# A hybrid decoder layer: attention values 13 or 14 steps behind their scores, eight heads in one softmax, norm weights moved into the rotary tables and the keys

## The chip, the core and the metric

The kernel runs on one core of one Trainium2 chip. The core has a matrix engine (PE, with its weight loads shown as PEld), a vector engine (DVE), a scalar engine (ACT), a general engine (POOL) and SP, which here only issues DMAs. Each engine works through its own instructions in order; they wait for one another through semaphores. Times are device microseconds of one execution, from repeated runs of the same program. The profile comes from one further execution that was recorded by the hardware.

## The reference

One layer of a decoder on 256 tokens of width 2048, in float32. The part that matters here is the attention half of the first mixing block: 32 query heads of 64 dimensions, 8 key and value heads, a window of 128 tokens in two blocks of 128 queries, and a learned sink per head.

```python
qh = _rmsnorm(q.reshape(b, s, ATT_HEADS, ATT_HEAD_DIM), q_norm_g[i])
kh = _rmsnorm(k.reshape(b, s, ATT_KV_HEADS, ATT_HEAD_DIM), k_norm_g[i])
qh = _partial_rope(qh, cos, sin)
kh = _partial_rope(kh, cos, sin)
...
sc = jnp.einsum('bnqhrd,bnkhd->bnhrqk', qb, kb) * scale
sc = jnp.where(mask[None, :, None, None], sc, -jnp.inf)
m = jnp.maximum(jnp.max(sc, axis=-1, keepdims=True), sink)
e = jnp.exp(sc - m)
pr = e / (jnp.sum(e, axis=-1, keepdims=True) + jnp.exp(sink - m))
o = jnp.einsum('bnhrqk,bnkhd->bnqhrd', pr, vb)
```

Around it stand the state-space half of the same block, the output projection that both halves feed, a gated feed-forward part and a small embedding part.

## The kernel before

Nearly all the work is products of 256 token rows with big float32 weights. Each weight tile of 128x1024 is loaded into a raw buffer `w` (`WR` = 6 of them), then split into a high part `wh` (a cast on ACT, L192) and the rest `wl` (a subtraction on DVE, L193), with `WB` = 4 buffers each. One such tile is one **step**: twelve matmuls of 128x512 on PE (L219 to L221: high by high, low weights by high, high weights by low, for two k tiles and two token blocks). A raw buffer comes free when DVE has made `wl` from it; `wh` and `wl` come free when PE has done their step.

The attention stage is written as 104 steps, numbered from 0, and PE's order in it is written by hand: q(0) is steps 0 to 7, the keys 8 to 15, the values' projection 16 to 23, q(1) 24 to 31, output(1) 32 to 39, q(2) 40 to 47, output(2) 48 to 55, q(3) 56 to 63, and output(3) to output(7) fill steps 64 to 103. A table `at` hangs the attention products behind certain steps. The other engines' order is set by a scheduler.

The queries come in four groups j of eight heads, two key heads (kv) each. For each group and each block b of 128 queries the chain is this:

- `norm_rope` takes the projected queries from the accumulators (ACT, L607), squares them (ACT, L609), sums per head (DVE, L611), takes the power -1/2 on POOL (L187, called from `rstd`), scales (DVE, L613), multiplies by the norm's weights (POOL, L614, 128x512), and turns the first 16 dimensions (POOL, six small instructions, L621 to L623).
- `flipped` transposes float32 through its two 16-bit halves: a copy into `half` (POOL for queries and keys, ACT for probabilities), a DMA transpose issued by SP (L631), and a copy from `flip` on POOL (L632). The result is `qT`, `kT`, or the probabilities `s` themselves, transposed in place. There are two `half` and two `flip` buffers for all of them.
- `scores(j, b, kv)` makes four heads: PE (L679) into one PSUM tile `sc`, mask added on DVE (L680), maximum (L687), minimum with the sink (L688), four exponentials on ACT (L691), the denominator (L693 to L696), the scaling (DVE, L697), then `flipped`. A group takes four such calls, two with 128 keys (b = 0) and two with 256 (b = 1).
- `values(j)` multiplies the transposed probabilities with `v` on PE (L712) and splits the result into `yT`, the left side of output(4 + j).

SP issues weight loads (L207) and transposes (L631) from one queue, in order. A projection's result is added from its accumulators to the residual by DVE (L359); there are two pairs of accumulators, so PE can start a block of two steps when DVE has added the block before the last.

Of the kernel before, what the change touches and what calls it, by code (L numbers as in the profile page):

```python
# [20 lines left out]
P = 128  # L21
# [6 lines left out]
KG = 4  # L28
KW = 2
WB = 4  # L30
WR = 6
LINE = 512

HD = 64
# [31 lines left out]
def hybrid_layer(  # L66
# [64 lines left out]
    hp = ctx.enter_context(tc.tile_pool(name="hp", bufs=1))  # L131
    hres = [sb(hp, [P, D], f"h{b}") for b in range(NB)]
    mix = ExitStack()
    yp_ = mix.enter_context(tc.tile_pool(name="yp", bufs=4))
    xin_ = ExitStack()
    xin = xin_.enter_context(tc.tile_pool(name="xin", bufs=1))
    gn = sb(const, [P, 4 * KT], "gains")
# [151 lines left out]
    def v3(a, m):  # L289
        return a.rearrange("p (a b) -> p a b", a=m)  # L290
# [308 lines left out]
    with tc.tile_pool(name="att_s", bufs=2) as as_, tc.tile_pool(name="att", bufs=2, reuse_waits="tile") as ap_, tc.tile_pool(name="ps_sc", bufs=1, space=PSUM) as ps_sc:  # L599
# [2 lines left out]
        nsink = sb(as_, [P, 32], "nsink", bufs=1)  # L602
        V.tensor_scalar_mul(nsink, sink, -1.0)

        def norm_rope(acc, b, gain, tag):
            r = sb(ap_, [P, NC], "qkr", bufs=1)
            S.activation(out=r, in_=acc[b], func=AF.Copy, scale=rx[:, b : b + 1])  # L607
            n = sb(ap_, [P, NC], "qkn")
            S.activation(out=n, in_=r, func=AF.Square)  # L609
            ss = sb(as_, [P, 8], "ss8")  # L610
            V.tensor_reduce(out=ss, in_=v3(n, 8), axis=AX.X, op=ALU.add)  # L611
            rs = rstd(ss, HD, 8, "rs8")
            V.tensor_tensor(out=v3(r, 8), in0=v3(r, 8), in1=bc(rs, HD), op=ALU.mult)  # L613
            G.tensor_tensor(out=v3(n, 8), in0=v3(r, 8), in1=gain.unsqueeze(1).to_broadcast([P, 8, HD]), op=ALU.mult)  # L614
            n3 = v3(n, 8)
            a, c_ = n3[:, :, :HALF], n3[:, :, HALF:ROPE]
            cs = cos_t[:, b, :].unsqueeze(1).to_broadcast([P, 8, HALF])
            sn = sin_t[:, b, :].unsqueeze(1).to_broadcast([P, 8, HALF])
            t = [sb(as_, [P, 8, HALF], f"rot{i}", bufs=1) for i in range(4)]
            for i, (u_, w_) in enumerate(((a, cs), (c_, sn), (c_, cs), (a, sn))):  # L620
                G.tensor_tensor(out=t[i], in0=u_, in1=w_, op=ALU.mult)  # L621
            G.tensor_tensor(out=a, in0=t[0], in1=t[1], op=ALU.subtract)
            G.tensor_tensor(out=c_, in0=t[2], in1=t[3], op=ALU.add)  # L623
            return n

        def flipped(dst, n, put):

# [11 lines left out]
        def queries(j, acc):  # L639
            qTs[j] = []  # L640
            for b in range(NB):
                n = norm_rope(acc, b, qscaled, "q")
# [5 lines left out]

        def keys(acc):
            for b in range(NB):  # L650
                n = norm_rope(acc, b, kg_, "k")
# [15 lines left out]

        probs = {}

        def scores(j, b, kv):  # L670

            W = (b + 1) * P
            qT = qTs[j][b]
            s = sb(ap_, [P, 4, W], f"s{b}")
            sc = ps_sc.tile([P, 4, 2 * P], F32, tag="sc", name=nm("sc"))[:, :, :W]
            for i in range(2):
                for e in range(2):
                    es = slice(e * HD, (e + 1) * HD)
                    PE.matmul(sc[:, 2 * e + i, :], lhsT=qT[es, kv * 2 + i, :], rhs=kT[es, 2 * j + kv, :W], start=True, stop=True)  # L679
            V.tensor_tensor(out=s, in0=sc, in1=band[:, 2 * P - W :].unsqueeze(1).to_broadcast([P, 4, W]), op=ALU.add)  # L680
            h0 = j * 8 + kv * 4

            def pairs(a):
                return a[:, h0 : h0 + 4].rearrange("p (i e) -> p e i", e=2)

            nm_ = sb(as_, [P, 4], "nm")
            V.tensor_reduce(out=nm_, in_=s, axis=AX.X, op=ALU.max, negate=True)  # L687
            V.tensor_tensor(out=v3(nm_, 2), in0=v3(nm_, 2), in1=pairs(nsink), op=ALU.min)  # L688
            den = sb(as_, [P, 4], "den")
            for h in range(4):  # L690
                S.activation(out=s[:, h, :], in_=s[:, h, :], func=AF.Exp, bias=nm_[:, h : h + 1], accum_out=den[:, h : h + 1])  # L691
            es_ = sb(as_, [P, 4], "es")
            V.tensor_tensor(out=v3(es_, 2), in0=v3(nm_, 2), in1=pairs(sink), op=ALU.add)  # L693
            S.activation(out=es_, in_=es_, func=AF.Exp)
            V.tensor_tensor(out=den, in0=den, in1=es_, op=ALU.add)
            V.reciprocal(den, den)  # L696
            V.tensor_tensor(out=s, in0=s, in1=bc(den, W), op=ALU.mult)  # L697
            p = s.rearrange("p h w -> p (h w)")
            flipped(p.rearrange("p (c t) -> p c t", t=P), 4 * W, lambda half: S.copy(half, halves(p)))
            probs[j, b, kv] = s.rearrange("p h (k t) -> p h k t", t=P)  # L700

        def values(j):

            yT = Lhs(yp_, KG, "y")
            for b in range(NB):
                o = tr_tile()
                for kv in range(2):
                    pT = probs.pop((j, b, kv))
                    vs = slice((2 * j + kv) * HD, (2 * j + kv + 1) * HD)
                    for kb in range(b + 1):  # L710
                        for e in range(2):
                            PE.matmul(  # L712
                                v3(o[e * HD : (e + 1) * HD, kv * 2 * P : (kv + 1) * 2 * P], 2),
                                lhsT=v[kb][:, vs],
                                rhs=pT[:, 2 * e : 2 * e + 2, kb, :],
                                start=(kb == 0),
                                stop=(kb == b),
                                skip_group_check=True,
                            )
                hi, lo = (t[:, :, b * P : (b + 1) * P] for t in yT.t[0])  # L720
                split(v3(o, 4), hi, lo)
            held[4 + j] = (yT, w_out, 4 + j, 1)
# [211 lines left out]
```

## Time and profile before

| what | value |
|---|---|
| median of 3 runs | 1462.4 us (1461.29 to 1462.82) |
| the profiled execution | 1464.43 us, its span 1462.7 us |
| mean granted TensorE clock | 0.992 |
| ACT busy | 793.1 us (54%) |
| POOL busy | 307.1 us (21%) |
| HBM traffic | 268.32 MB read, 2.13 MB written |

The span is the time from the first to the last instruction in the trace; the execution's own time is 1.7 us more. Waits are listed by the engine that waits and by what came last; a wait counts for the total only where it is PE's, since PE is busy nearly all the time. Matmuls are pipelined: one of 128x512 is shown with 0.39 us, but the next one starts 0.23 us later, so their spacing is read from start to start.

### The profile page before, as it was taken

The page shows a single profiled execution, that of the slowest core. Times are in us where ns is not written, and L with a number is a line of the kernel's source. Part 1 is how long each engine was busy: PE and PEld are TensorE (multiplying, and loading weights), DVE is VectorE, ACT ScalarE, POOL GpSimd, SP SyncE. Part 2 cuts the span into 40 slices and gives each one's busy share as a digit, 9 for nine tenths or more (in the row PEclk, how much of TensorE's full clock was granted, in tenths as well). Part 3 has the DMA queues.
Part 4 walks back from the last instruction along what each step waited for, and adds up shares of the span by engine and source line. Part 5 has one row for each costly group of instructions (what it writes and reads, how often), then busy time and mean ns, then how long its engine had stood idle before and what let it go on. Part 6 is the DMA issues. An engine that isn't in the chain of part 4 may idle for free.

```text
span 1462.7 us, 18060 instructions
## 1 busy us (share of the span) xinstructions
PE 1431.3 (98%) x6516; PEld 1167.7 (80%) x6516; DVE 1000.7 (68%) x1262; ACT 793.1 (54%) x1075; POOL 307.1 (21%) x246
## 2 busy tenths in 40 slices
PE   9999999999979899999999999999999999999998
PEld 6787888888757667888888888888888888888887
DVE  6668876767868697775666755774675576476854
ACT  6675555544546564565655545544554564455653
POOL 0002010029444350102334202311320231020000
PEclk9999999999989999999999999999999999999999
DMA  9665665556875686758778768767776877676672
GB/s 336 211 190 184 201 189 172 174 158 200 200 191 148 189 199 167 207 185 226 209 211 221 215 197 217 214 204 204 211 222 196 212 209 216 202 211 188 212 221 85
DMA packets 163595, 292.62 MB, mean 200 GB/s; under 512 B 93169, under 2 KB 96049, under 8 KB 163121
## 3 DMA queue, kind: packets, MB, share of 16 engines
q1 hardware_dynamic: 163072, 290.99, 68.6%
q8 instruction: 51, 0.84, 0.2%
q10 hardware_dynamic: 432, 0.48, 0.1%
q14 instruction: 40, 0.32, 0.1%
HBM read 268.32 MB, written 2.13 MB: 185 GB/s over the span
## 4 chain that ended last, share of the span: by engine, by line
PE 88%; DMA 4%; DVE 4%; POOL 2%; ACT 1%; issue 1%; SPq 0%; DVEq 0%; POOLq 0%; ACTq 0%
PE acc L219 27%; PE acc L220 27%; PE acc L221 27%; DMA flip<-half 2%; DVE wl L193 1%; PE ms L495 1%; PE acc L318 1%; PE acc L319 1%; PE acc L317 1%; PE tr L252 1%; DMA w<-in_w_in_dram 1%; ACT wh L192 1%; PE tr L712 1%; POOL s L632 1%; PE sc L679 1%
## 5 line engine op out<-in xcount | busy, mean ns | idle before, releaser
L193 DVE TENSOR_TENSOR wl<-w,wh 128x1024 fp32r<-128x1024 f32 (+1 forms) x493 | 640.3, 1303 | 364.3 <-ACT wh L192 363.1
L192 ACT CAST wh<-w 128x1024 fp32r<-128x1024 f32 (+1 forms) x493 | 515.2, 1048 | 496.7 <-PE acc L221 446.6
L220 PE MATMUL acc<-wl,ah 128*128 128x512 f32 x1280 | 500.9, 391 | 1.4 <-DVE wl L193 1.4
L221 PE MATMUL acc<-wh,al 128*128 128x512 f32 x1280 | 500.6, 391 | 0.0
L219 PE MATMUL acc<-wh,ah 128*128 128x512 f32 x1280 | 499.9, 392 | 0.0
L220 PEld LDWEIGHTS acc<-wl,ah 128*128 128x128 f32 x1280 | 241.1, 188 | 52.2 <-DVE wl L193 2.2
L219 PEld LDWEIGHTS acc<-wh,ah 128*128 128x128 f32 x1280 | 241.1, 188 | 52.1 <-issue 2.4
L221 PEld LDWEIGHTS acc<-wh,al 128*128 128x128 f32 x1280 | 240.9, 188 | 50.2 <-issue 0.5
L221 PE MATMUL acc<-wh,gl 128*128 128x512 f32 x352 | 137.0, 389 | 0.0
L220 PE MATMUL acc<-wl,gh 128*128 128x512 f32 x352 | 137.0, 389 | 0.0
L219 PE MATMUL acc<-wh,gh 128*128 128x512 f32 x352 | 136.4, 389 | 0.0
L814 POOL COPY half<-u 128x1024 uint16<-128x1024 uint16 x44 | 61.4, 1407 | 262.5 <-ACT u L812 262.5
L219 PE MATMUL acc<-wh,yh 128*128 128x512 f32 x256 | 102.1, 399 | 1.9 <-DVE h L359 1.9
L220 PE MATMUL acc<-wl,yh 128*128 128x512 f32 x256 | 100.2, 391 | 0.0
L221 PE MATMUL acc<-wh,yl 128*128 128x512 f32 x256 | 99.8, 391 | 0.0
L817 POOL COPY uc<-flip 128x1024 uint16<-128x1024 uint16 x44 | 56.4, 1281 | 169.2 <-DMA flip<-half 169.2
L220 PEld LDWEIGHTS acc<-wl,gh 128*128 128x128 f32 x352 | 66.1, 188 | 13.7
L221 PEld LDWEIGHTS acc<-wh,gl 128*128 128x128 f32 x352 | 66.1, 188 | 13.7
L219 PEld LDWEIGHTS acc<-wh,gh 128*128 128x128 f32 x352 | 66.1, 188 | 13.6
L359 DVE TENSOR_TENSOR h<-h,acc 128x512 f32<-128x512 f32 x112 | 73.3, 678 | 3.6 <-PE acc L221 3.6
L268 DVE SCALAR_TENSOR_TENSOR cv<-uc,fcw,cv 128x254 f32<-128x254 f32 (+1 forms) x176 | 73.2, 477 | 3.4 <-ACT cv L266 3.4
L219 PEld LDWEIGHTS acc<-wh,yh 128*128 128x128 f32 x256 | 48.3, 189 | 16.2 <-issue 3.8
(225 smaller groups left out, 1160.4 us busy)
## 6 DMA issues: line engine op xcount, KB each, us to landing
w<-in_w_up_dram SPq DMA_DIRECT2D x176, 512.0 KB, 4.1
w<-in_w_in_dram SPq DMA_DIRECT2D x126, 512.0 KB, 4.1
w<-in_w_down_dram SPq DMA_DIRECT2D x88, 512.0 KB, 4.3
w<-in_w_out_dram SPq DMA_DIRECT2D x64, 512.0 KB, 4.2
w<-in_w_pg_dram SPq DMA_DIRECT2D x32, 512.0 KB, 4.3
seg<-scr SPq DMA_DIRECT2D x8, 512.0 KB, 5.1
xt<-in_xT_dram SPq DMA_DIRECT2D x16, 128.0 KB, 7.1
h<-in_x_dram SPq DMA_DIRECT2D x2, 1024.0 KB, 8.4
```

The source lines that it names most:

```text
L192: S.copy(hi, src)
L193: V.tensor_tensor(out=lo, in0=src, in1=hi.bitcast(F32), op=ALU.subtract)
L219: PE.matmul(acc[b], lhsT=hi, rhs=wh[:, i, :], start=(k == 0), stop=False)
L220: PE.matmul(acc[b], lhsT=hi, rhs=wl[:, i, :], start=False, stop=False)
L221: PE.matmul(acc[b], lhsT=lo, rhs=wh[:, i, :], start=False, stop=(k == total - 1))
L252: PE.transpose(tr[:, i, b * P : (b + 1) * P], src[b][:, f * P : (f + 1) * P], ident)
L268: V.scalar_tensor_tensor(out=dst[:, s:], in0=ps[:, : T - s], scalar=taps[n - 1 - s], in1=dst[:, s:], op0=ALU.mult, op1=ALU.add)
L317: PE.matmul(acc[b], lhsT=h, rhs=wh[:, c, :], start=(k == 0), stop=False)
L318: PE.matmul(acc[b], lhsT=h, rhs=wl[:, c, :], start=False, stop=False)
L359: V.tensor_tensor(out=hs, in0=hs, in1=acc[b], op=ALU.add)
L814: G.tensor_copy(half.rearrange("p (a n) -> p a n", a=2), u_.bitcast(U16).rearrange("p (n a) -> p a n", a=2))
L817: G.tensor_copy(uc[:, :, b * P : (b + 1) * P].bitcast(U16).rearrange("p f (t a) -> p f t a", a=2), flip.rearrange("p (a f) t -> p f t a", ...
```

## The change

The values' products move to later steps, and the scores to other steps; both blocks of two key heads at b = 0 are made as one softmax of eight heads; the queries' norm weights leave `norm_rope`.

```diff
-WR = 6
+WR = 7
...
-    yp_ = mix.enter_context(tc.tile_pool(name="yp", bufs=4))
+    yp_ = mix.enter_context(tc.tile_pool(name="yp", bufs=3))
...
+        def turned(table, gain, tag):
+            t = sb(as_, [P, NB, HALF], tag, bufs=1)
+            V.tensor_tensor(out=t, in0=table, in1=gain.unsqueeze(1).to_broadcast([P, NB, HALF]), op=ALU.mult)
+            return t
+        qa, qc = qscaled[:, :HALF], qscaled[:, HALF:ROPE]
+        qrope = [turned(t, g, f"qr{i}") for i, (t, g) in enumerate(((cos_t, qa), (sin_t, qc), (cos_t, qc), (sin_t, qa)))]
+        krope = [cos_t, sin_t, cos_t, sin_t]
+        kgain = sb(as_, [P, HD], "kgs", bufs=1)
+        V.tensor_copy(kgain[:, :ROPE], kg_[:, :ROPE])
+        V.tensor_tensor(out=kgain[:, ROPE:], in0=kg_[:, ROPE:], in1=qscaled[:, ROPE:], op=ALU.mult)
...
-            r = sb(ap_, [P, NC], "qkr", bufs=1)
+            r = sb(ap_, [P, NC], "qkr")
...
-            n = sb(ap_, [P, NC], "qkn")
+            n = sb(small, [P, NC], "hsq")
...
-            G.tensor_tensor(out=v3(n, 8), in0=v3(r, 8), in1=gain.unsqueeze(1).to_broadcast([P, 8, HD]), op=ALU.mult)
+            if gain is not None:
+                G.tensor_tensor(out=r3, in0=r3, in1=gain.unsqueeze(1).to_broadcast([P, 8, HD]), op=ALU.mult)
...
-        def scores(j, b, kv):
+        def scores(j, b, kvs):
...
-            s = sb(ap_, [P, 4, W], f"s{b}")
-            sc = ps_sc.tile([P, 4, 2 * P], F32, tag="sc", name=nm("sc"))[:, :, :W]
+            m = 2 * len(kvs)
+            s = sb(ap_, [P, 2 * m, W], f"s{b}", bufs=2 + b)
+            sc = ps_sc.tile([P, 2, 2 * NC // (2 * W), W], F32, tag="sc", name=nm("sc"))
...
-        for j, first_score, value in ((0, 29, 44), (1, 46, 60), (2, 62, 76), (3, 78, 92)):
-            for u in range(4):
-                at[first_score + 2 * u] = lambda j=j, u=u: scores(j, u // 2, u % 2)
+        for j, first, value in ((0, (30, 33, 36), 50), (1, (43, 46, 51), 65), (2, (58, 61, 66), 79), (3, (75, 77, 80), 93)):
+            for n, (b, kvs) in zip(first, ((0, (0, 1)), (1, (0,)), (1, (1,)))):
+                at[n] = lambda j=j, b=b, kvs=kvs: scores(j, b, kvs)
             at[value] = lambda j=j: values(j)
```

The last scores of the four groups stood behind steps 35, 52, 68 and 84 and now stand behind 36, 51, 66 and 80; the values stood behind 44, 60, 76 and 92, that is 9, 8, 8 and 8 steps later, and now stand behind 50, 65, 79 and 93, that is 14, 14, 13 and 13 steps later. The weights of the queries' norm are multiplied once into the rotary tables (dimensions 0 to 15) and into the keys' weights (dimensions 16 to 63, where queries and keys meet only in their product). The second block's probabilities have three buffers instead of two.

On PE, behind step 44, the first group's values stood between two products of q(2); the first two rows are block 0 (`tr` 3759), the other four block 1, and before it stands the last product of the step:

```order
L221 MATMUL acc_755_3666<-wh_3740,al_23_141 128x512
L712 MATMUL tr_3759<-s_664_3309,v_642_3195 64x256 x2
L712 MATMUL tr_3759<-s_701_3427,v_642_3195 64x256 x2
L712 MATMUL tr_3766<-s_716_3493,v_642_3195 64x256 x2
L712 MATMUL tr_3766<-s_716_3493,v_643_3197 64x256 x2
L712 MATMUL tr_3766<-s_731_3559,v_642_3195 64x256 x2
L712 MATMUL tr_3766<-s_731_3559,v_643_3197 64x256 x2
L219 MATMUL acc_754_3665<-wh_3778,ah_22_140 128x512
```

In the changed kernel the same products on PE stand behind step 50, inside output(2):

```order
L221 MATMUL acc_825_3955<-wh_3957,yl_418_2164 128x512
L731 MATMUL tr_3976<-s_672_3336,v_647_3204 64x256 x4
L731 MATMUL tr_3983<-s_714_3482,v_647_3204 64x256 x2
L731 MATMUL tr_3983<-s_714_3482,v_648_3206 64x256 x2
L731 MATMUL tr_3983<-s_734_3568,v_647_3204 64x256 x2
L731 MATMUL tr_3983<-s_734_3568,v_648_3206 64x256 x2
L219 MATMUL acc_824_3954<-wh_3995,yh_417_2163 128x512
```

The products are the same; they moved six steps later, and block 0 reads one tile of eight heads (`s` 672) where it read two.

On DVE, the end of the first group's softmax, among the splits of q(2)'s weights (`wl`), the denominator (`den`) and the sums into the residual (`h`); the scaling of the last probabilities is the row that writes `s` 731:

```order
L693 TENSOR_TENSOR es_3574<-nm_3566,rows_134 128x4
L359 TENSOR_TENSOR h_1_83<-h_1_83,acc_746_3625 128x512
L193 TENSOR_TENSOR wl_3705<-w_3703,wh_3704 128x1024
L359 TENSOR_TENSOR h_2_84<-h_2_84,acc_747_3626 128x512
L695 TENSOR_TENSOR den_3569<-den_3569,es_3574 128x4
L193 TENSOR_TENSOR wl_3723<-w_3721,wh_3722 128x1024
L696 RECIPROCAL den_3569<-den_3569 128x4
L697 TENSOR_TENSOR s_731_3559<-s_731_3559,den_3569 128x1024
L193 TENSOR_TENSOR wl_3741<-w_3739,wh_3740 128x1024
```

In the changed kernel the same place on DVE reads:

```order
L711 TENSOR_TENSOR es_3583<-nm_3575,rows_134 128x4
L193 TENSOR_TENSOR wl_3694<-w_3692,wh_3693 128x1024
L359 TENSOR_TENSOR h_1_83<-h_1_83,acc_744_3614 128x512
L359 TENSOR_TENSOR h_2_84<-h_2_84,acc_745_3615 128x512
L713 TENSOR_TENSOR den_3578<-den_3578,es_3583 128x4
L714 RECIPROCAL den_3578<-den_3578 128x4
L715 TENSOR_TENSOR s_734_3568<-s_734_3568,den_3578 128x1024
L193 TENSOR_TENSOR wl_3712<-w_3710,wh_3711 128x1024
```

The last scaling stood between the splits of steps 43 (`wl` 3723) and 44 (`wl` 3741), with the values behind step 44; it now stands between the splits of steps 42 (`wl` 3694) and 43 (`wl` 3712), with the values behind step 50.

On SP, the transposes at the end of the first group before (16 tiles for `s` with 256 keys, 8 for `qT` and for `s` with 128 keys), among the loads of steps 49 (`w` 3959) to 53; the first two of the four rows go with `qT` of group 1 and with block 0 of group 0, the other two with block 1 of group 0:

```order
L631 DMA_TRANSPOSE flip_3424<-half_3422 128x8x128
L631 DMA_TRANSPOSE flip_3450<-half_3448 128x8x128
L207 DMA w_3959<-in_w_out_dram 128x1024
L207 DMA w_3981<-in_w_out_dram 128x1024
L631 DMA_TRANSPOSE flip_3516<-half_3514 128x16x128
L207 DMA w_4025<-in_w_out_dram 128x1024
L207 DMA w_4047<-in_w_out_dram 128x1024
L631 DMA_TRANSPOSE flip_3582<-half_3580 128x16x128
L207 DMA w_4091<-in_w_out_dram 128x1024
```

In the changed kernel SP issues there, among the loads of steps 49 (`w` 3934) to 52, first `qT` of group 1 and then block 1 of group 0:

```order
L207 DMA w_3934<-in_w_out_dram 128x1024
L644 DMA_TRANSPOSE flip_3439<-half_3437 128x8x128
L644 DMA_TRANSPOSE flip_3505<-half_3503 128x16x128
L207 DMA w_3956<-in_w_out_dram 128x1024
L207 DMA w_3994<-in_w_out_dram 128x1024
L644 DMA_TRANSPOSE flip_3591<-half_3589 128x16x128
L207 DMA w_4042<-in_w_out_dram 128x1024
```

The last transpose of the group (`flip` 3582, now 3591) moved from behind the load of step 52 to behind that of step 51.

More of the change, by code (lines that the diff above doesn't have):

```diff
@@ L603, in hybrid_layer, with norm_rope @@
         V.tensor_scalar_mul(nsink, sink, -1.0)
-        def norm_rope(acc, b, gain, tag):
-            r = sb(ap_, [P, NC], "qkr", bufs=1)
+        def turned(table, gain, tag):
[8 more added lines that the diff above has]
+        V.tensor_tensor(out=kgain[:, ROPE:], in0=kg_[:, ROPE:], in1=qscaled[:, ROPE:], op=ALU.mult)
+        def norm_rope(acc, b, rope, gain=None):
+            r = sb(ap_, [P, NC], "qkr")
             S.activation(out=r, in_=acc[b], func=AF.Copy, scale=rx[:, b : b + 1])
-            n = sb(ap_, [P, NC], "qkn")
+            n = sb(small, [P, NC], "hsq")
             S.activation(out=n, in_=r, func=AF.Square)
@@ L612, in norm_rope @@
             rs = rstd(ss, HD, 8, "rs8")
[L613 to L618, printed above, removed]
+            r3 = v3(r, 8)
+            V.tensor_tensor(out=r3, in0=r3, in1=bc(rs, HD), op=ALU.mult)
+            if gain is not None:
+                G.tensor_tensor(out=r3, in0=r3, in1=gain.unsqueeze(1).to_broadcast([P, 8, HD]), op=ALU.mult)
+            a, c_ = r3[:, :, :HALF], r3[:, :, HALF:ROPE]
             t = [sb(as_, [P, 8, HALF], f"rot{i}", bufs=1) for i in range(4)]
-            for i, (u_, w_) in enumerate(((a, cs), (c_, sn), (c_, cs), (a, sn))):
-                G.tensor_tensor(out=t[i], in0=u_, in1=w_, op=ALU.mult)
+            for i, u_ in enumerate((a, c_, c_, a)):
+                G.tensor_tensor(out=t[i], in0=u_, in1=rope[i][:, b, :].unsqueeze(1).to_broadcast([P, 8, HALF]), op=ALU.mult)
             G.tensor_tensor(out=a, in0=t[0], in1=t[1], op=ALU.subtract)
             G.tensor_tensor(out=c_, in0=t[2], in1=t[3], op=ALU.add)
-            return n
+            return r
         def flipped(dst, n, put):
@@ L641, in queries @@
             for b in range(NB):
-                n = norm_rope(acc, b, qscaled, "q")
+                n = norm_rope(acc, b, qrope)
                 qT = sb(ap_, [P, 4, P], f"qT{b}")
@@ L650, in keys @@
             for b in range(NB):
-                n = norm_rope(acc, b, kg_, "k")
+                n = norm_rope(acc, b, krope, kgain)
                 def twice(half):
@@ L668, in hybrid_layer @@
         probs = {}
-        def scores(j, b, kv):
+        def scores(j, b, kvs):
             W = (b + 1) * P
+            m = 2 * len(kvs)
             qT = qTs[j][b]
-            s = sb(ap_, [P, 4, W], f"s{b}")
-            sc = ps_sc.tile([P, 4, 2 * P], F32, tag="sc", name=nm("sc"))[:, :, :W]
[L676 to L681, printed above, removed]
+            s = sb(ap_, [P, 2 * m, W], f"s{b}", bufs=2 + b)
+            sc = ps_sc.tile([P, 2, 2 * NC // (2 * W), W], F32, tag="sc", name=nm("sc"))
+            for kv in kvs:
+                for i in range(2):
+                    for e in range(2):
+                        es = slice(e * HD, (e + 1) * HD)
+                        PE.matmul(
+                            sc[:, e, (kv - kvs[0]) * 2 + i, :], lhsT=qT[es, kv * 2 + i, :], rhs=kT[es, 2 * j + kv, :W], start=True, stop=True
+                        )
+            sc = sc.rearrange("p e m w -> p (e m) w")
+            V.tensor_tensor(out=s, in0=sc, in1=band[:, 2 * P - W :].unsqueeze(1).to_broadcast([P, 2 * m, W]), op=ALU.add)
+            h0 = j * 8 + kvs[0] * 4
             def pairs(a):
-                return a[:, h0 : h0 + 4].rearrange("p (i e) -> p e i", e=2)
-            nm_ = sb(as_, [P, 4], "nm")
+                return a[:, h0 : h0 + 2 * m].rearrange("p (m e) -> p e m", e=2)
+            nm_ = sb(as_, [P, 2 * m], "nm")
             V.tensor_reduce(out=nm_, in_=s, axis=AX.X, op=ALU.max, negate=True)
             V.tensor_tensor(out=v3(nm_, 2), in0=v3(nm_, 2), in1=pairs(nsink), op=ALU.min)
-            den = sb(as_, [P, 4], "den")
-            for h in range(4):
+            den = sb(as_, [P, 2 * m], "den")
+            for h in range(2 * m):
                 S.activation(out=s[:, h, :], in_=s[:, h, :], func=AF.Exp, bias=nm_[:, h : h + 1], accum_out=den[:, h : h + 1])
-            es_ = sb(as_, [P, 4], "es")
+            es_ = sb(as_, [P, 2 * m], "es")
             V.tensor_tensor(out=v3(es_, 2), in0=v3(nm_, 2), in1=pairs(sink), op=ALU.add)
@@ L698, in scores @@
             p = s.rearrange("p h w -> p (h w)")
-            flipped(p.rearrange("p (c t) -> p c t", t=P), 4 * W, lambda half: S.copy(half, halves(p)))
-            probs[j, b, kv] = s.rearrange("p h (k t) -> p h k t", t=P)
+            flipped(p.rearrange("p (c t) -> p c t", t=P), 2 * m * W, lambda half: S.copy(half, halves(p)))
+            for kv in kvs:
+                probs[j, b, kv] = [s[:, e * m + (kv - kvs[0]) * 2 :, :][:, :2].rearrange("p h (k t) -> p h k t", t=P) for e in range(2)]
         def values(j):
@@ L714, in values @@
                                 lhsT=v[kb][:, vs],
-                                rhs=pT[:, 2 * e : 2 * e + 2, kb, :],
+                                rhs=pT[e][:, :, kb, :],
                                 start=(kb == 0),
```

## The prediction

> **What bounds the kernel.** I read the page's first part, then PE's waits, then the attention stage by stretches.
>
> ```profile
> span 1462.7 us, 18060 instructions
> PE 1431.3 (98%) x6516; PEld 1167.7 (80%) x6516; DVE 1000.7 (68%) x1262; ACT 793.1 (54%) x1075; POOL 307.1 (21%) x246
> ```
>
> PE is busy for all but 31.4 us of the span. Nothing in the change takes matmul work away, so only PE's idle time, and time in which it runs slowly, can be won.
>
> ```profile
> PE tr L712 <- POOL s L632: 19.2, 6, 5.1
> PE acc L219 <- DVE h L359: 1.9, 1, 1.9
> ```
>
> Of the idle time 19.2 us in six waits belong to the values' products (L712), which wait for the last copies of transposed probabilities on POOL (L632). One wait of 1.9 us is for accumulators that DVE had not yet added to the residual. The rest is spread over the start and other stages, which the change leaves as they are.
>
> The next rows are PE's own timeline around the four groups of values: start, duration, and in brackets the idle time ahead. The last row of each group is the eighth product after them (j = 0, 1, 2, 3 from the top).
>
> ```profile
> 421.34 1.08 PE L712 MATMUL tr<-s,v 128*64 128x256 f32 x8
> 426.64 1.10 PE L712 MATMUL tr<-s,v 128*64 128x256 f32 x8 [4.22 <-POOL s L632]
> 432.85 1.97 PE L712 MATMUL tr<-s,v 128*64 128x256 f32 x8 [5.10 <-POOL s L632]
> ...
> 437.88 0.40 PE L220 MATMUL acc<-wl,ah 128*128 128x512 f32 x1
> ...
> 484.26 1.08 PE L712 MATMUL tr<-s,v 128*64 128x256 f32 x8
> ...
> 496.18 0.39 PE L220 MATMUL acc<-wl,ah 128*128 128x512 f32 x1
> ...
> 542.54 1.08 PE L712 MATMUL tr<-s,v 128*64 128x256 f32 x8
> ...
> 554.82 0.39 PE L220 MATMUL acc<-wl,yh 128*128 128x512 f32 x1
> ...
> 601.17 2.81 PE L712 MATMUL tr<-s,v 128*64 128x256 f32 x24
> ...
> 605.65 0.40 PE L220 MATMUL acc<-wl,yh 128*128 128x512 f32 x1
> ```
>
> Group 3 shows the price without a wait: 605.65 - 601.17 = 4.48 us from the first values' product to the eighth product behind them. Group 0 took 437.88 - 421.34 = 16.54, group 1 11.92, group 2 12.28. So the waits cost 12.06 + 7.44 + 7.80 = **27.3 us**, which is 8.1 more than the idle time: after the long waits the same eight values' products take 1.97 instead of 1.08 us, and the products behind them start more slowly for a while.
>
> [...]
>
> **The change, part by part.**
>
> *Values later.* Does a group's last probability arrive in the new distance? I need PE's step, and the price of what stands between.
>
> ```profile
> 415.81 0.39 PE L219 MATMUL acc<-wh,ah 128*128 128x512 f32 x1
> ...
> 421.02 0.39 PE L221 MATMUL acc<-wh,al 128*128 128x512 f32 x1
> ```
>
> These are 23 products apart: 0.2265 us each, **2.72 us a step** of twelve.
>
> ```profile
> 380.37 0.71 PE L679 MATMUL sc<-kT,qT 64*128 64x128 f32 x8
> ...
> 395.57 1.13 PE L679 MATMUL sc<-kT,qT 64*128 64x256 f32 x8
> ...
> 448.17 0.71 PE L679 MATMUL sc<-kT,qT 64*128 64x128 f32 x8
> 454.49 1.14 PE L679 MATMUL sc<-kT,qT 64*128 64x256 f32 x8
> 461.21 1.13 PE L679 MATMUL sc<-kT,qT 64*128 64x256 f32 x8
> ...
> 519.49 1.13 PE L679 MATMUL sc<-kT,qT 64*128 64x256 f32 x8
> ...
> 578.12 1.13 PE L679 MATMUL sc<-kT,qT 64*128 64x256 f32 x8
> ```
>
> Scores of 128 keys cost 6.32 - 2 steps = 0.88 us (448.17 to 454.49), of 256 keys 6.72 - 2 steps = 1.28. Eight heads of 128 keys in one call are not in the trace; two of the small ones bound it from above with 1.76, one from below with 0.88. I take 1.76: the matmuls are the same. A group of values costs 4.48 - 7 x 0.2265 = 2.89.
>
> The last copies of each group on POOL show when the probabilities were there:
>
> ```profile
> 430.68 2.11 POOL L632 COPY s<-flip 128x2048 uint16<-128x2048 uint16 x1 [4.09 <-DMA flip<-half]
> 489.22 2.11 POOL L632 COPY s<-flip 128x2048 uint16<-128x2048 uint16 x1 [2.46 <-DMA flip<-half]
> 548.36 2.12 POOL L632 COPY s<-flip 128x2048 uint16<-128x2048 uint16 x1 [1.39 <-DMA flip<-half]
> 599.03 2.15 POOL L632 COPY s<-flip 128x2048 uint16<-128x2048 uint16 x1 [1.20 <-DMA flip<-half]
> ```
>
> From the last scores to the end of these copies: group 0 432.8 - 395.6 = 37.2 us, group 1 30.1, group 2 31.0, group 3 23.1. The new distance is the last scores themselves (1.28), the steps, and the other scores that stand between: group 0, 14 steps with the calls behind 43 and 46: 1.28 + 38.08 + 1.76 + 1.28 = 42.4; group 1 the same, 42.4; group 2, 13 steps, 39.7; group 3, 13 steps, 36.6. **Margins 5.2, 12.3, 8.7 and 13.5 us**, even at the old latencies. All three groups that waited stop waiting: -27.3 us. What was late next, the residual's use of `yT`, is not near: output(7) starts two steps after the last values, 5.4 us, where it had three, and PE's waits name none there.
>
> *Scores earlier.* The scores of groups 1 to 3 stand three to four steps nearer to their queries. The last copies into `qT`, for the groups 1, 1, 2, 3:
>
> ```profile
> 404.59 1.16 POOL L632 COPY qT<-flip 128x1024 uint16<-128x1024 uint16 x1 [4.09 <-DMA flip<-half]
> 416.61 1.16 POOL L632 COPY qT<-flip 128x1024 uint16<-128x1024 uint16 x1 [3.78 <-DMA flip<-half]
> 476.56 1.82 POOL L632 COPY qT<-flip 128x1024 uint16<-128x1024 uint16 x1 [6.45 <-DMA flip<-half]
> 534.54 2.21 POOL L632 COPY qT<-flip 128x1024 uint16<-128x1024 uint16 x1 [6.06 <-DMA flip<-half]
> ```
>
> The projection of group 1 ends at 380.37, with the scores that stood behind its last step; that of group 2 ends one step before the scores at 448.17, at 445.45. Block 0 of group 1 was ready 25.4 us later and is now wanted 12 steps and two calls later, 35.2 us. Block 1 of group 1 took 37.4 and is wanted after 15 steps and three calls, 45.1. Block 1 of group 2 took 32.9 and is wanted after 14 steps, two calls and the values, 44.0; group 3 is like it. [...]
>
> *One softmax of eight heads, and no multiplication of the queries.* The first two rows are stretches of the stage (length, then busy time of PE, PEld, DVE, ACT and POOL, then the granted clock, the DMA share and GB/s); the others group the instructions from 372 to 612 us.
>
> ```profile
> 372.00:612.00 240.00, 218.90 (x1025) 167.78 (x1024) 187.01 (x253) 133.44 (x248) 88.31 (x77) 0.95 0.69 184
> ...
> 558.00:612.00 54.00, 54.00 (x263) 42.34 (x262) 46.90 (x65) 31.65 (x59) 7.66 (x4) 1.00 0.76 194
> L614 POOL TENSOR_TENSOR qkn<-qkr,qgs 128x512 f32<-128x512 f32 x6 | 11.7, 1958 | 7.4 <-DVE es L693 3.7 <-DVE den L696 3.7
> L680 DVE TENSOR_TENSOR s<-sc,band 128x1024 f32<-128x1024 f32 x8 | 9.7, 1211 | 0.0
> L680 DVE TENSOR_TENSOR s<-sc,band 128x512 f32<-128x512 f32 x8 | 5.4, 680 | 3.2 <-PE sc L679 3.2
> ```
>
> DVE is busy 187.0 of 240 us there. Two additions of 512 become one of 1024: 2 x 0.68 - 1.21 = 0.15 us saved a group; maximum and scaling likewise, and four small instructions of about 0.2 go, so about 1.5 us a group, 6 in all. POOL loses 1.96 us from each of six query blocks here (and two before). None of it is on PE; it shortens the chains above, and I take it as margin: 0, between 0 and the 1.9 us wait for accumulators. The six small multiplications of tables and weights that DVE gains at the start stand beside an unbroken PE; they cost nothing.
>
> *Seven raw buffers, three `y` buffers.* Weight loads move one step ahead of the transposes; values(0) takes the buffer of output(1), which is done eleven steps earlier. Nothing in PE's waits names a weight load here: 0.
>
> **Sum.** The profiled execution took 1464.43 us, 2.0 over the median of 1462.4. 1464.4 - 27.3 = 1437.1, or 1435.1 at the median. PE now runs without its three rests, so DVE has 181 us of work in 240 - 29 = 211, 86% instead of 78%. I therefore keep the wait for accumulators and add one more of the same price, 1.9: **1437.0 us**.
>
> **Rivals.**
>
> *A wait remains.* Group 0 has the thinnest margin, 5.2 us, and its chain shares DVE and the two `half` buffers with group 1's queries. Should its copies come 10 us later than before, it keeps 5 us of idle and about 2.7 of slow clock; at worst all of its 12.1. That gives 1441 to 1449. Against it: the last scaling now stands one split earlier on DVE, and there are three calls instead of four.
>
> *The waits only change place.* If the scores of each group wait for `qT` as the values did for `s`, PE loses about 27 us again: 1459 to 1465. It would need `qT` to come 8 to 16 us later than it did; for it speaks only that transposes of both kinds share SP's queue.
>
> *Slower.* DVE becomes the bound: each block of output() needs the accumulators that DVE freed two steps before, and DVE is in order, so a block's sum can stand behind an addition, a maximum and a POOL power. The price is 1.9 us each time, and it decides once 15 of the 28 blocks of output(1) to output(7) wait (15 x 1.9 = 28.5 > 27.3). With 20 waits the time is 1435.1 + 38 = 1473. The trace speaks against it: one such wait in the whole stage, and none from 558 to 612 us, where DVE was busy for 46.9 of 54 us, 87%, and PE did not rest.
>
> **How the numbers follow.** The forecast has 0.76, a remaining wait 0.15, no gain 0.04, slower 0.05. The range reaches from no wait for accumulators at all (1435.1 - 1.9), 1433, into the rival of a remaining wait, 1447. A measurement of this kernel can tell about 0.2%, 2.9 us, from no change: faster 0.93 (the first two and half of the third), same 0.02, slower 0.05.
>
> **What would show it.** PE's list of waits loses the row of values on POOL; the eighth product stands 4.5 us behind the first values' product in all four groups; values' products take no 1.97 us. Scores that wait for POOL's `qT`, or several rows of accumulators waiting for DVE, would show the rivals. I am wrong if the chain from scores to copies grows beyond 40 us in the new order.

## The result and the profile after

| | before | after |
|---|---|---|
| median, us | 1462.6 (1461.3 to 1463.7) | **1436.0** (1435.0 to 1437.0, 4 runs) |
| ratio to before | | 0.9819, 95% interval 0.9802 to 0.9836 |
| the profiled execution, its span, us | 1464.4, 1462.7 | 1435.8, 1434.1 |
| mean granted TensorE clock | 0.992 | 0.999 |

The changed kernel takes 26.6 us less, 1.8%. The forecast was 1437.0. The first lines of the page of the kernel after:

```profile
span 1434.1 us, 18053 instructions
PE 1421.9 (99%) x6516; PEld 1166.2 (81%) x6516; DVE 995.0 (69%) x1240; ACT 792.0 (55%) x1067; POOL 288.2 (20%) x234
```

The span is 28.6 us shorter. PE's idle time went from 31.4 to 12.2 us (1434.1 - 1421.9), so 19.2 of it; the other 9.4 are PE's busy time, though it does the same number of matmuls. PE's waits after, over the whole span (engine and line that waits, what it waits for, us in all, times, longest):

```profile
PE acc L317 <- ACT wh L192: 1.9, 2, 1.3
PE acc L220 <- DVE wl L193: 1.8, 2, 1.2
...
PE acc L219 <- DVE h L359: 0.8, 1, 0.8
PE sc L694 <- DVE s L698: 0.6, 1, 0.6
```

The row of the values on POOL, 19.2 us before, is gone; nothing over 2 us is left. In PE's timeline after, the four groups of values and some scores stand like this (start, duration, the idle time ahead in brackets where there is any):

```profile
376.80 1.16 PE L694 MATMUL sc<-kT,qT 64*128 64x128 f32 x16
...
386.28 1.14 PE L694 MATMUL sc<-kT,qT 64*128 64x256 f32 x8
...
437.70 2.81 PE L731 MATMUL tr<-s,v 128*64 128x256 f32 x24
...
442.16 0.39 PE L220 MATMUL acc<-wl,yh 128*128 128x512 f32 x1
...
473.19 1.14 PE L694 MATMUL sc<-kT,qT 64*128 64x256 f32 x8
...
485.36 2.81 PE L731 MATMUL tr<-s,v 128*64 128x256 f32 x24
...
530.97 2.81 PE L731 MATMUL tr<-s,v 128*64 128x256 f32 x24
...
575.32 2.81 PE L731 MATMUL tr<-s,v 128*64 128x256 f32 x24
```

Each group is one unbroken piece of 24 products now, without a bracket and without the slow 1.97 us. From the first values' product of group 0 to the eighth product behind it are 442.16 - 437.70 = 4.46 us, where they were 16.54. Eight heads in one call cost 386.28 - 376.80 - 3 x 2.72 = 1.32 us. The stretch from 372 to 612 us, in the columns of before (PE, PEld, DVE, ACT, POOL, clock, DMA share, GB/s):

```profile
372.00:612.00 240.00, 238.06 (x1163) 188.53 (x1162) 204.28 (x253) 149.40 (x275) 75.45 (x68) 1.00 0.75 203
```

PE is busy for 238.06 of 240 us, at a granted clock of 1.00, where it was 218.90 at 0.95; DVE for 204.28. These are the last copies of each group's probabilities on POOL, and between them the copy into `qT` for block 1 of group 2:

```profile
420.24 2.14 POOL L645 COPY s<-flip 128x2048 uint16<-128x2048 uint16 x1 [3.25 <-DMA flip<-half]
...
471.57 1.16 POOL L645 COPY qT<-flip 128x1024 uint16<-128x1024 uint16 x1 [12.80 <-DMA flip<-half]
473.36 2.90 POOL L645 COPY s<-flip 128x2048 uint16<-128x2048 uint16 x1 [0.63 <-PE acc L221]
...
523.53 2.13 POOL L645 COPY s<-flip 128x2048 uint16<-128x2048 uint16 x1 [3.99 <-DMA flip<-half]
...
564.73 2.15 POOL L645 COPY s<-flip 128x2048 uint16<-128x2048 uint16 x1 [11.14 <-DMA flip<-half]
```

The probabilities were ready 15.3, 9.1, 5.3 and 8.4 us before the values of groups 0 to 3 (437.70 - 422.38, and so on). The `qT` row is the near miss of this kernel: ready at 472.73, used by the scores at 473.19. Only 0.46 us were to spare.

### The profile page after: what moved, and what is told of

Read it like the earlier page. It is cut to its first block, busy times and chain, and to the rows that moved or that the text cites. A ratio compares the mean times of both kernels' runs of the same rounds, so it can differ in the third digit from the quotient of the medians.

```text
span 1434.1 us, 18053 instructions
## 1 busy us (share of the span) xinstructions
PE 1421.9 (99%) x6516; PEld 1166.2 (81%) x6516; DVE 995.0 (69%) x1240; ACT 792.0 (55%) x1067; POOL 288.2 (20%) x234
## 4 chain that ended last, share of the span: by engine, by line
PE 61%; DVE 1%; issue 0%; ACT 0%; DVEq 0%
PE acc L220 20%; PE acc L221 20%; PE acc L219 20%; PE tr L252 0%; DVE wl L193 0%; PE tr L731 0%; DVE h L359 0%; DVE den L713 0%; DVE sg L883 0%; ACT s L709 0%; DVE yl L193 0%; DVE s L698 0%; DVE nm L705 0%; DVE sg L884 0%; ACT sg L882 0%
## 5 line engine op out<-in xcount | busy, mean ns | idle before, releaser
L220 PEld LDWEIGHTS acc<-wl,gh 128*128 128x128 f32 x352 | 66.1, 188 | 13.7
L221 PEld LDWEIGHTS acc<-wh,gl 128*128 128x128 f32 x352 | 66.1, 188 | 13.7
```

The lines of the kernel that those rows point to most:

```text
L220: PE.matmul(acc[b], lhsT=hi, rhs=wl[:, i, :], start=False, stop=False)
L221: PE.matmul(acc[b], lhsT=lo, rhs=wh[:, i, :], start=False, stop=(k == total - 1))
```

## Experiments: where the time came from

Twelve kernels ran, one of them the kernel after once more, in three batches. The kernel before, run beside them, had medians of 1462.7, 1463.1 and 1462.1 us. In the diffs a tuple of the table is (group, (steps of the three calls of scores), step of the values).

**Values at their old distance.** Everything of the change, but each group's values five or six steps earlier, so that they stand 8 or 9 steps behind their last scores.

```diff
-for j, first, value in ((0, (30, 33, 36), 50), (1, (43, 46, 51), 65), (2, (58, 61, 66), 79), (3, (75, 77, 80), 93)):
+for j, first, value in ((0, (30, 33, 36), 45), (1, (43, 46, 51), 59), (2, (58, 61, 66), 74), (3, (75, 77, 80), 88)):
```

> The changed kernel with the values' products back at the old distances behind their last scores: steps 45, 59, 74 and 88 (9, 8, 8 and 8 steps). Theory 'distance': the change's gain is the longer distance, so the waits come back. From the changed kernel's own trace the last copies end 26.7, 32.9, 34.6 and 30.2 us after the last scores, and these distances are 27.1, 24.4, 23.0 and 23.0 us: waits of 0, 8.5, 11.5 and 7.1 us, and about 2.7 us of slow clock behind each of the three, 1471 us; if the other engines' new order shortens the chains to what they were before, down to 1455. Theory 'less work': the merged softmax, the queries' multiplication that is gone and the seventh buffer are what ended the waits, and the distance is not needed: 1436 to 1442.

1452.3 us (1450.7 to 1456.6), ratio 0.9934 (0.9917 to 0.9951): 16 of the 26.6 us are gone. The row of before is back among PE's waits:

```profile
PE tr L731 <- POOL s L645: 13.3, 2, 8.2
```

Two groups wait now, not three, as PE's timeline of this kernel shows:

```profile
424.37 2.81 PE L731 MATMUL tr<-s,v 128*64 128x256 f32 x24
...
471.52 1.95 PE L731 MATMUL tr<-s,v 128*64 128x256 f32 x16
478.53 1.97 PE L731 MATMUL tr<-s,v 128*64 128x256 f32 x8 [5.07 <-POOL s L645]
...
525.85 1.95 PE L731 MATMUL tr<-s,v 128*64 128x256 f32 x16
536.01 1.98 PE L731 MATMUL tr<-s,v 128*64 128x256 f32 x8 [8.22 <-POOL s L645]
```

Group 0 no longer waits even at the short distance: in the kernel after its chain from the last scores to the last copy takes 26.7 us, not 37.2, so the other parts of the change shortened it. Here it takes 29.2 us, and the copy is done at 425.45, 0.7 us before the first product that reads it. Group 0's share of the gain has two causes, and either alone removes its wait. The distance theory had priced group 0 at nothing too; its lower bound of 1455 fits the waits of groups 1 and 2 that the old chains would give (30.1 - 24.4 and 31.0 - 23.0, together 13.7 us) with a slow spell of 2.7 us, a third of the 8.1 us of before, behind each. The profiled execution, with 13.3 us of waits, took 1456.6 us. The four executions reach from 1450.7 to that, and why their median lies below the bound is not shown.

**Values three steps earlier.** If only the wait counts, and not the distance as such, three steps fewer must cost nothing.

```diff
-for j, first, value in ((0, (30, 33, 36), 50), (1, (43, 46, 51), 65), (2, (58, 61, 66), 79), (3, (75, 77, 80), 93)):
+for j, first, value in ((0, (30, 33, 36), 47), (1, (43, 46, 51), 62), (2, (58, 61, 66), 76), (3, (75, 77, 80), 90)):
```

> The changed kernel with the values' products three steps (8.2 us) earlier: 47, 62, 76, 90. [...] Theory 'every step counts': moving 3 of 5 steps back gives back about half of the gain, 1447 to 1452.

1436.7 us (1435.3 to 1437.7), ratio 0.9822 (0.9805 to 0.9838), no wait of the values: group 2's chain, which with the 34.6 us of the kernel after would have been 2.9 us late, took 31.3 us here. It is a threshold. One row is new:

```profile
PE sc L694 <- POOL qT L645: 1.4, 1, 1.4
```

It stands before the first scores of group 2, those of block 0: their `qT` was there at 466.86, and PE used it at 466.92. In the kernel after it is there at 456.78 for scores at 463.71. The near miss of above, block 1 of the same group, is not what waited; it had 3.35 us to spare (473.06 for 476.41).

**The kernel before, with its values later only.** The old softmax of four heads, the old scores, the multiplication on POOL; buffers of `s` and `yp` as the longer life of the probabilities needs them.

```diff
-s = sb(ap_, [P, 4, W], f"s{b}")
+s = sb(ap_, [P, 4, W], f"s{b}", bufs=4 - 2 * b)
...
-((0, 29, 44), (1, 46, 60), (2, 62, 76), (3, 78, 92))
+((0, 29, 49), (1, 46, 65), (2, 62, 81), (3, 78, 93))
```

> The kernel before with the later values alone: 49, 65, 81 and 93, that is 14, 13, 13 and 9 steps behind the last scores; four buffers for the probabilities of block 0 and three y buffers instead of two and four, which the later values need. Scores, softmax, norm weights and six raw buffers as before. Theory 'distance': 1462.6 - 27.3 = 1435, and up to 1440 with the wait for accumulators and the four-head calls that stay. Theory 'less work': with the old chains DVE has no rest any more and falls behind; values or accumulators wait, 1445 to 1462.

1438.0 us (1436.5 to 1438.7), ratio 0.983 (0.9815 to 0.9845). The distance alone gives 24.6 of the 26.6 us. All the rest of the change is worth 2.0 us beside it (3.6 against a second measurement of the kernel after, below), and the intervals overlap.

**Four heads a call again.** The kernel after, with the first block's softmax made in two calls of four heads, as before, but one step apart, where the kernel before has two steps between them.

```diff
-(0, (30, 33, 36), 50), (1, (43, 46, 51), 65), (2, (58, 61, 66), 79), (3, (75, 77, 80), 93)
+(0, (30, 31, 33, 36), 50), (1, (43, 44, 46, 51), 65), (2, (58, 59, 61, 66), 79), (3, (75, 76, 77, 80), 93)
...
-((0, (0, 1)), (1, (0,)), (1, (1,)))
+((0, (0,)), (0, (1,)), (1, (0,)), (1, (1,)))
```

> The changed kernel with block 0's eight heads again as two softmaxes of four, behind steps 30 and 31, 43 and 44, 58 and 59, 75 and 76 (four buffers of half the size). Theory 'distance': PE pays for the extra break only; eight heads in one call cost 1.32 us in the changed kernel's trace (9.48 us from 376.80 to 386.28, less three steps) where two calls cost 2 x 0.88: 0.4 us a group, 1.8 us in all, 1437 to 1439. Theory 'less work': DVE has 1.5 us more a group and PE waits for it again, 1441 to 1450.

1440.8 us (1439.6 to 1442.3), ratio 0.9851 (0.9836 to 0.9865): between the two expectations. PE's timeline has one wait that the kernel after has not:

```profile
416.57 0.71 PE L694 MATMUL sc<-kT,qT 64*128 64x128 f32 x8
423.35 1.22 PE L694 MATMUL sc<-kT,qT 64*128 64x128 f32 x8 [3.11 <-DVE s L697]
```

There is one PSUM tile `sc`, and the second call needs it back from DVE's addition for the first, which stood behind two splits on DVE (418.39 to 422.62). With two steps between the calls, as in the kernel before with its values later, there is no such wait. Behind the wait the same eight products take 1.22 instead of 0.71 us, and the products behind them start 0.43 instead of 0.23 us apart: from these scores over a whole step to the next product are 429.73 - 423.35 = 6.38 us, where scores and a step took 0.88 + 2.72 = 3.60 before. The granted clock from 372 to 612 us is 0.99, in the kernel after 1.00. The page has 5.5 us more of busy PE than after and the same idle time of 12.1 us (other short waits came out 3 us shorter):

```profile
span 1439.5 us, 18104 instructions
PE 1427.4 (99%) x6516; PEld 1168.4 (81%) x6516; DVE 1002.5 (70%) x1268; ACT 793.0 (55%) x1075; POOL 292.4 (20%) x238
```

Of the 5.5 us 1.8 are the extra calls (four times 1.76 - 1.32), as the theory 'distance' had it; 6.38 - 3.60 = 2.8 are what the slow clock takes; the other 0.9 were not told apart. So 1.8 us are the price of the calls themselves. The wait and its slow clock, which neither expectation had, come from calls one step apart on one PSUM tile; two calls two steps apart beside the rest of the change were not run.

**Smaller parts.** Six raw buffers instead of seven; and the scores of group 2's block 1, and of group 3, one step later, to give the near miss room.

```diff
-WR = 7
+WR = 6
```

> The changed kernel with six raw weight buffers instead of seven. Theory 'no part in it': no wait of PE names a weight load, 1436 +- 0.7. Rival 'head of line': with one load less ahead, a transpose that waits for its copy holds up a load that PE needs, or the loads' order makes queries late: 1438 to 1445.

```diff
-(2, (58, 61, 66), 79), (3, (75, 77, 80), 93)
+(2, (58, 62, 66), 79), (3, (75, 78, 81), 93)
```

> The changed kernel with the second scores of groups 2 and 3 one step later (62 instead of 61, 78 instead of 77) and the last of group 3 behind 81 instead of 80. The changed kernel's PE waits 0.55 us for DVE's addition before the scores behind step 77, and 0.75 and 0.63 us soon after. If these come from calls two steps apart on DVE, they go: 1434.1 to 1435.3. If DVE's backlog moves along, nothing changes: 1436 +- 0.7; if the last probabilities of group 3 come late (12 steps then, 33.9 us, where the trace needs 30.2), it is slower by up to 2 us.

> The changed kernel once more, beside the next ones on the same chip: 1436.0 us, ratio 0.982.

Six buffers took 1435.6 us (1434.7 to 1440.4), the later scores 1434.8 (1433.1 to 1435.5), the kernel after itself, run again beside them, 1434.4 (1433.5 to 1439.0). None of the three can be told from the others. The seventh buffer plays no part that these runs can show.

**The multiplication of the queries back on POOL.** The tables and the keys' weights are plain again, and POOL multiplies each block of queries by the norm's weights, as before. All else is the kernel after.

```diff
-n = norm_rope(acc, b, qrope)
+n = norm_rope(acc, b, krope, qscaled)
...
-n = norm_rope(acc, b, krope, kgain)
+n = norm_rope(acc, b, krope, kg_)
```

> The changed kernel with the multiplication by the queries' norm weights back on POOL (128x512, 1.96 us a block in the trace of before), keys with their own weights, rotary tables without them. In the changed kernel's trace the transposed queries of group 2, block 1, are there at 472.73 us and PE uses them at 473.19: 0.46 us to spare. Theory 'near miss': two blocks of 2 us on POOL in a row make them 2 to 4 us late, and PE's scores wait 1.5 to 3.5 us in that group (others have 3 us or more to spare): 1437.5 to 1441. Theory 'hidden': the transposes are held by SP's order and not by POOL, nothing is late: 1436 +- 0.7.

1455.2 us (1452.6 to 1456.1), ratio 0.9942 (0.993 to 0.9955): about 20 us more than the kernel after, far outside both expectations. Eight small multiplications off PE undo three quarters of the gain. PE's waits of this kernel from 372 to 612 us:

```profile
PE sc L694 <- POOL qT L645: 4.4, 1, 4.4
PE acc L219 <- DVE h L359: 3.2, 4, 1.6
PE acc L220 <- DVE wl L193: 2.5, 3, 1.4
PE acc L219 <- ACT wh L192: 1.5, 1, 1.5
PE sc L694 <- DVE s L698: 1.3, 1, 1.3
PE acc L219 <- ACT es L712: 1.1, 1, 1.1
```

One wait for `qT`, and ten short ones for five other things. The wait is for block 0 of group 2, not for block 1, the near miss. All but one of the short ones come after ACT was held at 416 us; these are rows of the timelines of ACT and of DVE of the same kernel:

```profile
421.38 1.90 ACT L717 COPY half<-s 128x2048 uint16<-128x2048 uint16 x1 [4.94 <-DMA flip<-half]
...
424.26 2.21 DVE L193 TENSOR_TENSOR wl<-w,wh 128x1024 fp32r<-128x1024 f32 x1 [6.13 <-ACT wh L192]
```

ACT wants to copy probabilities into `half`, but both `half` buffers are still being transposed, one of them for the queries that came 8 us later than in the kernel after (`qT` copied at 421.33 instead of 413.05). ACT is in order, so the weight casts behind that copy are late, DVE has nothing to split for 6.13 us, and it runs behind from there.

The multiplication itself takes 1.29 us of these 8. The scheduler answered it by moving other work: DVE scales the second block of group 1's queries behind four more splits. The first of these rows of DVE's timeline is from the kernel after, the second from this one:

```profile
388.26 0.82 DVE L628 TENSOR_TENSOR qkr<-qkr,rs 128x512 f32<-128x512 f32 x1
...
398.58 0.68 DVE L628 TENSOR_TENSOR qkr<-qkr,rs 128x512 f32<-128x512 f32 x1
```

SP then issues the transpose at 416.27, behind four weight loads, where the kernel after does it at 408.00 behind two.

Three more kernels and a control took this apart. Those with a third buffer or a spare one have six raw buffers, to make room; above, six and seven came out alike.

```diff
-half = sb(ap_, [P, 2, n], "half", U16)
+half = sb(ap_, [P, 2, n], "half", U16, 3)
```

First that line with the multiplication back, then that line alone in the kernel after:

> The kernel after with the queries' multiplication back on POOL, a third buffer of half, and six raw buffers (which six_raw_buffers showed to play no part). query_multiplication_back took 1455.2; its trace shows ACT's copy of probabilities held 4.94 us at 421.38 because both half buffers still wait for transposes, and the weight casts behind it on ACT late. If the shared half buffers are the cause: 1436 to 1442, and no wait of ACT for a transposed half over 2 us between 415 and 480 us. If it is something else, as the place that the scheduler gives the scaling of group 1's second block on DVE (behind the 129th split there, behind the 125th in the kernel after): 1450 to 1457.

> The kernel after with a third buffer of half and six raw buffers, and nothing else: the control for mult_back_third_half. The kernel after has no wait of PE that names a transposed half, so both theories expect 1434 to 1438, a tie with it.

With the multiplication 1442.8 us (1442.0 to 1443.9), ratio 0.9866 (0.985 to 0.9883); the control without it 1434.5 (1432.7 to 1436.4), ratio 0.9811, no better than the kernel after. The third buffer gives back 12.4 us where the multiplication is there, and nothing where it is not. PE's waits with the multiplication and three buffers, from 372 to 612 us, are down to two:

```profile
PE sc L694 <- POOL qT L645: 5.7, 1, 5.7
PE acc L219 <- DVE h L359: 0.8, 1, 0.8
```

What is left is the wait for `qT` of group 2. POOL's timeline shows how it came about:

```profile
447.05 1.30 POOL L630 TENSOR_TENSOR qkr<-qkr,qgs 128x512 f32<-128x512 f32 x1 [2.33 <-ACT yh L192]
...
450.86 1.29 POOL L630 TENSOR_TENSOR qkr<-qkr,qgs 128x512 f32<-128x512 f32 x1
454.34 2.31 POOL L645 COPY s<-flip 128x2048 uint16<-128x2048 uint16 x1 [2.19 <-DMA flip<-half]
...
459.69 2.03 POOL L657 COPY half<-qkr 128x1024 uint16<-128x1024 uint16 x1
...
470.07 1.15 POOL L645 COPY qT<-flip 128x1024 uint16<-128x1024 uint16 x1 [3.11 <-DMA flip<-half]
```

Between block 0's multiplication and its copy into `half` POOL also does block 1's multiplication and rotation, and waits 2.19 us for a transpose of probabilities, in order. The copy into `half`, at 459.69 here, is at 447.86 in the kernel after. PE's timeline has the price of that one wait:

```profile
471.27 2.08 PE L694 MATMUL sc<-kT,qT 64*128 64x128 f32 x16 [5.74 <-POOL qT L645]
...
477.23 0.39 PE L219 MATMUL acc<-wh,ah 128*128 128x512 f32 x1
```

From these scores to the tenth product behind them are 477.23 - 471.27 = 5.96 us. In the kernel after, without a wait, the same scores and ten products read:

```profile
463.71 1.16 PE L694 MATMUL sc<-kT,qT 64*128 64x128 f32 x16
...
466.98 0.39 PE L219 MATMUL acc<-wh,ah 128*128 128x512 f32 x1
```

That is 3.27 us, so 2.69 go to the slow clock: the products behind the late scores start 0.43 us apart, in the kernel after 0.23, and the granted clock from 415 to 480 us is 0.95, there 1.00. 5.74 + 2.69 = 8.4 us, and the medians of the two kernels differ by 1442.8 - 1434.5 = 8.3. The two profiled executions differ by more, 10.9 us (spans of 1441.8 and 1430.9).

Then the multiplication back with two `half` buffers, but with the scores of groups 1 to 3 two or three steps later:

```diff
-(1, (43, 46, 51), 65), (2, (58, 61, 66), 79), (3, (75, 77, 80), 93)
+(1, (46, 49, 54), 68), (2, (61, 64, 69), 83), (3, (77, 79, 82), 93)
```

> The kernel after with the queries' multiplication back, and the scores of the groups 1, 2, 3 at 46, 49, 54; 61, 64, 69; 77, 79, 82 (three, three and two steps later), the values at 68, 83 and 93. If the multiplication hurts because scores follow their queries three steps too near, as before_values_later (the same multiplication, later scores, 1438.0) suggests: 1436 to 1442. If its harm is on POOL or DVE whatever the scores' place: 1450 to 1457.

1440.3 us (1439.0 to 1441.8), ratio 0.9851 (0.9836 to 0.9865). No wait for `qT`; the largest that is left in the stage is one of 2.1 us for DVE's addition to scores. So the same multiplication costs 20 us with the scores near their queries and about 5 with the scores where they were, nearly. ACT is held at the two `half` buffers here as well, for 5.08 us before a copy at 421.90, and DVE has nothing to split for 6.27 us; but PE does not wait from 407 to 493 us. Of these two kernels the hold costs time only in the one whose scores stand near.

Last, the kernel after with a multiplication of the same size that nothing reads:

```diff
+spare = sb(as_, [P, NC], "spare", bufs=1)
+G.tensor_tensor(out=v3(spare, 8), in0=v3(n, 8), in1=qscaled.unsqueeze(1).to_broadcast([P, 8, HD]), op=ALU.mult)
```

> The kernel after (weights in the tables), six raw buffers, and the same multiplication of 128x512 on POOL for each block of queries, but into a spare buffer that nothing reads, behind the rotation: POOL does as much as in query_multiplication_back, its scheduler puts the scaling of group 1's second block on DVE behind the 129th split as there, but the data's chain is 2 us shorter. If the 2 us in the chain are what hurts: 1435 to 1440. If the place on DVE or POOL's time hurts: 1448 to 1457.

1442.8 us (1442.2 to 1443.5), ratio 0.9867 (0.9853 to 0.9882): between the two expectations. PE's waits from 372 to 612 us:

```profile
PE acc L220 <- DVE wl L193: 3.4, 3, 1.8
PE acc L219 <- DVE h L359: 2.0, 4, 0.8
PE sc L696 <- DVE s L700: 1.2, 1, 1.2
```

The wait for `qT` is gone, the short ones are not. So the 2 us in the data's chain make the wait for `qT`, and the short waits come without them, from POOL's time or from the place of the scaling of group 1's second block of queries on DVE, which the scheduler puts behind the 129th split in this kernel as in all with the multiplication (399.71 us here). ACT is held at `half` for 3.11 us here too, before a copy at 419.74. Which of these was not told apart, and no run has this kernel with a third buffer.

## Why the prediction was right, by its steps

**Values later, -27.3 us: right.** The idle time fell by 19.2 us, the very size of the row that was to vanish, and the kernel before with its values later gives 24.6 us by itself. The 9.4 us of PE's busy time are about the slow clock's 8.1 and what the eight-head calls save, 1.8 (together 9.9); the granted clock rose from 0.992 to 0.999. In the kernel before it is 0.50 in three spells of 10.24, 6.83 and 6.83 us, with PE busy for 5.14, 4.46 and 5.29 of them; half of that, an estimate of 7.4, is most of the 8.1. That the length of a wait tells whether the clock falls is not shown. In group 0 the values' products behind the wait of 4.22 us still took 1.10 us, those behind 5.10 took 1.97; but the granted clock fell 0.94 us after the wait of 4.22 had ended, and in groups 1 and 2 it fell with waits of 3.49 and 3.40 us. The 2.7 us of slow clock that the rival "a wait remains" adds are a third of the 8.1. The starts of the products gave 1435.1 at the median, before any new wait; measured were 1436.0 and, in the second measurement, 1434.4.

**Margins of the values: right in sign, wrong one by one.** Predicted were 5.2, 12.3, 8.7 and 13.5 us for groups 0 to 3; measured 15.3, 9.1, 5.3 and 8.4. The step assumed old latencies. Group 0's chain fell from 37.2 to 26.7 us, the others grew from 30.1, 31.0 and 23.1 to 32.9, 34.6 and 30.2. The thinnest group was to be 0, and was 2. That all margins stayed positive though three chains grew was in part luck.

**Queries' margins: the weakest step.** By the prediction's latencies and distances the smallest was 45.1 - 37.4 = 7.7 us, in group 1, and the sum has no term for the earlier scores; in the kernel after it is 0.46, in block 1 of group 2, for which the numbers gave 11.1 (44.0 - 32.9). Here too the old latency was taken over, and that no wait came of it was luck. Block 0 of group 2 was not priced at all. It had 6.9 us to spare in the kernel after, and it is the one that waited in the experiments above. SP works its queue in order, and put this transpose behind five weight loads; its rows in the kernel after (SPq is SP's queue):

```profile
457.89 6.90 SPq L207 DMA_DIRECT2D w<-in_w_out_dram  x5
464.89 6.23 SPq L644 DMA_TRANSPOSE flip<-half  x2
```

`half` had been ready since 458.77, and POOL waited until 471.57. The rival "the waits only change place" needed `qT` 8 to 16 us later, and was given 0.04. With the multiplication left in, the time came near that rival (1455.2 us), but only one group's scores waited for `qT`, 4.4 us; the other waits were short and for other things.

**The multiplication at 0: right as a term, wrong as a judgment.** Measured from the kernel before, nothing was lost by taking it as margin. But with scores this near it is worth 20 us: 12.4 that a third `half` buffer gives back, so by ACT held at the shared buffers and what queues behind it, and 8.3 that stay, with the wait for `qT`. How much of either belongs to the multiplication's own time, and how much to the scaling that the scheduler moved by 10.3 us, stays open. It is the part of the change that lets the scores stand earlier. What the earlier scores earn by themselves is little: the kernel before with its values later has the old scores, the old softmax and the multiplication, and is 2 to 4 us behind.

**Eight heads in one call at 0 on PE: mis-sized.** For the margins the bound from above, 1.76 us, was taken; a call took 1.32, so four calls save 1.8 us on PE, where the sum had 0. DVE's total fell by 5.7 us (1000.7 to 995.0), where 6 were predicted.

**Waits for accumulators, two of 1.9: not borne out.** One of 0.8 is left in the profiled execution. From 372 to 612 us PE rests for 1.9 us in all, where the forecast had kept 3.8. Without the added 1.9 the sum is 1435.1, between the two measurements, though it lacks the 1.8 us of the eight-head calls too. The rival of a bound DVE did not occur, though DVE is busy for 85% of that stretch (204.28 of 240; the prediction had 86%).

**Raw buffers at 0: right.** Six do as well as seven.

## What to carry to other kernels

Read the slack of a consumer, not only its waits: a distance in steps is worth its price only up to the point at which the wait is gone, and three steps fewer then cost nothing here. When several edits move work closer together, re-read every in-order queue and shared buffer between producer and consumer (here SP's, POOL's, and two `half` buffers for two kinds of data), since latencies measured in the old order did not carry over (the chains of groups 0 and 3 went from 37.2 and 23.1 us to 26.7 and 30.2). A small operation on an idle engine costs nothing while it has slack, and can cost more than its own length once it holds another engine that feeds the busy one, or makes the scheduler move other work: here eight multiplications of 1.3 to 2.3 us on POOL cost 20 us.

## What the runs showed of the hardware

- The rests of PE cost more than their length (27.3 us for 19.2 of idle time before, 8.4 for 5.74 with the multiplication and three `half` buffers), and the length of one wait did not tell whether the clock fell. In the traces of the kernels before and after all changes of the granted clock lie whole multiples of 3.41 us apart: 0.50 for 10.24, 6.83 and 6.83 us in the first and for 3.41 in the second, and 1.00 for 51.20 us between the spells of the first. Three stretches of the kernel before, in the columns of above:

```profile
420.76:424.17 3.41, 1.66 (x11) 0.67 (x9) 1.91 (x2) 3.41 (x5) 0.79 (x1) 1.00 0.94 238
424.17:427.58 3.41, 0.94 (x8) 0.48 (x8) 3.41 (x2) 0.43 (x1) 2.42 (x1) 1.00 0.79 198
427.58:437.82 10.24, 5.14 (x17) 3.25 (x16) 1.39 (x3) 0.59 (x1) 2.11 (x1) 0.50 0.59 157
```

  The wait of 4.22 us lies across the first two. PE was busy for 1.66 us of the first, and the clock stayed full; for 0.94 of the second, and it fell. With these two traces cut into stretches of 3.41 us in the same way, the clock fell behind all six that had full clock and PE busy for 1.48 us or less, and behind none with 1.66 or more; at half it stayed behind the four with 1.94 or less, and came back behind the four with 3.35 or more. In the kernel with the multiplication back, two waits of 1.54 and 1.40 us stand 0.50 us apart, and the products behind them start 0.43 instead of 0.23 us apart, up to 441.48.

- One such slow spell was measured by itself, 2.69 us; before, three cost 8.1, which is 2.7 each. The three lasted 10.24, 6.83 and 6.83 us, and PE was busy for only 0.17, 1.05 and 1.94 us of their first 3.41, which still held a part of the waits.
